# Late weight fetches, traced product order, single PSUM banks and early projection rows in a two-layer encoder trunk

## The chip, the cores and the metric

The kernel runs on one core of a Trainium2 chip. The metric is the device time of one execution in microseconds. A core has five engines with instruction queues of their own: TensorE (PE) does matmuls into PSUM, eight banks of 128 partitions x 512 fp32; VectorE (DVE), ScalarE (ACT) and GpSimd (POOL) work elementwise; SyncE (SP) issues the DMAs. Each engine works through its queue in the order in which it was written, and waits on semaphores for the others.

## The reference

The input is 1024 tokens of width 1024 in fp32. Two layers, each a mixer and an MLP with residuals, and a final RMSNorm:

```
for layer in range(2):
    mixer = even_mixer if layer == 0 else odd_mixer
    x = x + mixer(rmsnorm(x, g), ...)
    x = x + sq_relu_mlp(rmsnorm(x, g), w1, w2)     # u = relu(h @ w1); (u * u) @ w2, 4096 wide
return rmsnorm(x, g)
```

The even mixer is windowed attention beside a pooling mixer. The odd mixer is dense latent attention with 8 heads (`yc`, the first 512 channels) beside a gated recurrence (`yd`, the other 512), both concatenated and multiplied by `o_w_out` (1024 x 1024).

## The kernel before

Activations lie transposed, channels on the partitions, as tiles of 128 x 1024 (`G` tiles, 41 buffers); a half of one is `H2` or `U`. To keep fp32 accuracy each operand is split into a rounded part h and a rest l (`split`: a cast on ScalarE or POOL, a subtraction on VectorE or POOL), and each product runs three matmuls: h·h, h·l, l·h.

**Weights of the projections and of the MLP's last two pairs** go through one list, `wreq`, built by `requests` for all phases in order (L137), and two functions:

```
def weight(self, ahead=2):
    self.fetch(ahead + 1)
    return self.wout.pop(0)
```

`fetch` (L168) takes the next request, issues its DMA into one of two `raw` buffers, and splits it into two tiles of the tag `w`, of which there are eight. So when a phase takes its last weight, the first two of the next phase are already asked for. The tag `w` also holds the weight blocks of the MLP (`block("wb", ...)`, L272) and, in the odd attention, the transposed probabilities `cpT` (L1352) and the value tiles `VS` (L1317).

**The MLP** (`mlp`, L363) treats the 32 chunks of the hidden width in 16 pairs. 14 pairs use a seven-product scheme of 2 x 2 blocks (Strassen's kind), the last two (`TAIL`, pairs 14 and 15) do so only in the first products; their second products are plain and use four weights from `wreq` (L551). The first products of a pair go into four banks a, b, c, d: `head` writes a (B11), `rest` writes b (t2), c (t3), d (T1), then `second()` = `turn` calls `head2`, a second product into a (B21), then a second product into c (t4) and into d (B22). A product is 12 matmuls of 128 x 512. Between them VectorE and ScalarE read the banks: L396 copies a, L407 reads b, L410 and L419 read c, L412 and L424 read d, L401 reads a after `head2`. A second product into a bank must wait until the first result has been read. For the first six pairs (`NS`), `head` and `head2` run earlier, in a start stage, interleaved with the making of the operand blocks (`SNorm.late`, L1530), and `rest` follows for these six without `turn`. Pairs take two sets of banks in turn (`banks`, L284): four single-bank tiles of the pools `pb` and `pa`, or two double tiles `PS2` of the pool `p2`, cut into halves. `second` (L491) then runs the second products in three groups of pairs, seven steps per group, with `stream2` (weight blocks) and `tin` (hidden blocks read back from DRAM) prepared three ahead.

**The odd attention** (`odd`, L917) makes 128 steps u = 0 to 127, four for each of 32 (head, query pair): parts P (preparing a later head), S (scores of two query pairs ahead, in `PS2`), T (four transposes of probabilities to `cpT`) and V (`av`, the products with the values, `ODD_LAG` = 4 steps behind). After the loop the recurrence's output `yd` is split (L1164), the residual is loaded (`load_x`), the last four `av` run, `yc` is split, and then come the output rows: for each half n of the tokens and each of eight row blocks m, 24 matmuls over k = 4 to 7 (`yd`) and then k = 0 to 3 (`yc`).

**Order.** The source gives instructions in a traced order, but a planner with a cost model and the number of buffers of each tag reorders the instructions of every engine: an instruction that it thinks ready may pass earlier ones. `pin` (L111) ties an instruction behind the one traced before it on its engine. The numbers of buffers are kept as written; a tile waits until its buffer is free. `PS` (L92) hands out banks in rotation: two of `pb`, two of `pa`, and four halves of two `PS2` tiles; in `wide` mode the first four only.

Of the kernel before, what the change touches and what calls it, by code (L numbers as in the profile page):

```python
# [15 lines left out]
P = 128  # L16
S = 1024
# [29 lines left out]
class Trunk:  # L47
    def __init__(self, tc, a, pools, phases):
        self.tc, self.nc, self.a = tc, tc.nc, a
        self.cst, self.gp, self.wp, self.tp, self.sm, self.pb, self.pa, self.p2, self.dr = pools  # L50
# [10 lines left out]
        self.half = None  # L61
        self.halves = {}
        self.wreq = []
        self.wout = []
        for ph in phases:
            self.wreq += self.requests(ph)
# [21 lines left out]

    def PS2(self, name):
        return self.p2.tile([P, S], F32, tag="bb", name=self.nm(name))  # L90

    def PS(self, name):  # L92

        k = self.pk
        self.pk = (k + 1) % (4 if self.wide else 8)
        return self.PB(name) if k < 2 else self.PA(name) if k < 4 else self.PS2H(name)

    def PS2H(self, name):

        if self.half is None:  # L100
            self.half = self.PS2(name)
            return self.half[:, :N2]
        h, self.half = self.half, None
        return h[:, N2:]

    def set_wide(self, w):
        self.wide = w
        self.pk = 0
        self.half = None
# [27 lines left out]
    def requests(self, ph):  # L137
        a = self.a
        if ph == "even":
            r = [(a["e_w_in"][i], S) for i in (4, 5, 0, 1, 2, 3)] + [(a["e_w_pool"], N2)]  # L140
            r += [(a["e_w_in"][i], S) for i in (9, 8, 7, 6)]
            r += [(a["e_w_out"][1][m], S, "act", "pool") for m in range(4)]
            return r + [(a["e_w_out"][0][m], S) for m in range(4)]
        if ph == "odd":
            idx = {"xr3": 6, "ckv": 2, "cq0": 0, "cq1": 1, "xg0": 7, "xg1": 8, "xg2": 9, "xg3": 10}
            late = {"kn": (a["w_uk"], N2), "qr": (a["w_uq_r"], N2), "qn": (a["w_uq_n"], S), "vn": (a["w_uv"], N2)}
            r = [(a["o_w_in"][i], S, "act" if i != 5 else "pool") for i in (3, 4, 5)]
            seen = set()
            for op in ODD_START:
                k = op[:-1]  # L150
                if k in seen:
                    continue
                seen.add(k)
                if k in idx:
                    r.append((a["o_w_in"][idx[k]], S, "pool"))
                elif k in late:
                    r.append(late[k])
            return r + [(a["o_w_out"][m], S, "act", "pool") for m in range(NC)] * 2
        if ph == "final":
            return []  # L160
        l = int(ph[-1])
        return [(a["w2"][l, f], S) for p in TAIL for f in pair(p)]
# [5 lines left out]
    def fetch(self, ahead):  # L168

        while self.wreq and len(self.wout) < ahead:  # L170
            src, n, *eng = self.wreq.pop(0)
            raw = self.wp.tile([P, S], F32, tag="raw", name=self.nm("raw"), bufs=RAW_BUFS)
            self.nc.sync.dma_start(raw[:, :n], src)
            h = self.wp.tile([P, S], F32R, tag="w", name=self.nm("wh"))
            l = self.wp.tile([P, S], F32R, tag="w", name=self.nm("wl"))
            self.split(h[:, :n], l[:, :n], raw[:, :n], *eng)
            self.wout.append((h, l))

# [105 lines left out]
    def banks(self, which):  # L284
        if which:
            two = [self.PS2("q"), self.PS2("q")]
            return [x[:, s] for x in two for s in (slice(0, N2), slice(N2, S))]
        return [self.PB("q"), self.PB("q"), self.PA("q"), self.PA("q")]
# [74 lines left out]
    def mlp(self, l, nb, nxt, dram):  # L363
# [7 lines left out]
        def product(ps, blocks, first, last):  # L371
            w = stream.take()
            for c in range(4):
                x = blocks[c]
                cs = slice(c * P, (c + 1) * P)
                lo = slice(N2 + c * P, N2 + (c + 1) * P)
                for i, (a, b) in enumerate(((w[:, cs], x[:, :N2]), (w[:, cs], x[:, N2:]), (w[:, lo], x[:, :N2]))):
                    nc.tensor.matmul(ps, a, b, start=(first and c == 0 and i == 0), stop=(c == 3 and i == 2),  # L378
                                     skip_group_check=True)
# [12 lines left out]
        def head(p, ps):  # L392

            t1, u11 = self.U("t1"), self.U("u11")
            product(ps, nb.T["B11"], True, False)
            nc.scalar.copy(t1, ps)  # L396
            return t1, u11

        def head2(p, ps, u11):
            product(ps, nb.T["B21"], False, True)  # L400
            nc.scalar.activation(u11, ps, AF.Relu)  # L401
            nc.scalar.activation(u11, u11, AF.Square)
            put(p, "B11", u11)

        def rest(p, b, c, d, t1, u11, second=None):
            product(b, nb.T["t2"], True, False)
            V.tensor_tensor(t1, b, t1, op=ALU.add)  # L407
            product(c, nb.T["t3"], True, False)
            u22 = self.U("u22")
            V.tensor_tensor(u22, c, t1, op=ALU.subtract)  # L410
            product(d, nb.T["T1"], True, False)
# [5 lines left out]
            product(c, nb.T["t4"], False, True)  # L417
# [4 lines left out]
            product(d, nb.T["B22"], False, True)  # L422
# [30 lines left out]
        def turn(p, a, u11):  # L453
            head2(p, a, u11)
# [24 lines left out]
        for p in range(NS, NP):  # L479
            a, b, c, d = self.banks(k)  # L480
            k = 1 - k
            t1, u11 = head(p, a)
# [22 lines left out]
        for g, pairs in enumerate(GROUPS):  # L505
# [21 lines left out]
            A = self.banks(k)  # L527
            second(A, pairs, True, False)
# [388 lines left out]
    def odd(self, nb, xs, nxt):  # L917
# [217 lines left out]

        prep = iter(())
        for u in range(4 * NS):
            i, kk = divmod(u, 4)
            h, p = steps[i]
            for op in ODD_STEP:  # L1140
# [13 lines left out]
                elif op == "P":  # L1154
                    if p == 0 and kk == 0 and 1 <= h < 7:
                        prep = prep_qk(h + 1)
                    next(prep, None)
            if p == 1 and kk == 3 and h < 7:
                VS[h + 1] = self.head_values(h + 1, Vn)
        Yh, Yl = [None] * 8, [None] * 8  # L1160
        for c in range(4):
            Yh[4 + c], Yl[4 + c] = self.G("yh", F32R), self.G("yl", F32R)
            for s in H2:
                self.split(Yh[4 + c][:, s], Yl[4 + c][:, s], yd[c][:, s], "act", "pool")  # L1164
# [522 lines left out]
def trunk(tc, a, phases=("even", "mlp0", "odd", "mlp1", "final")):  # L1687
    PSUM = bass.MemoryType.PSUM
    with tc.tile_pool(name="cst", bufs=1) as cst, tc.tile_pool(name="sm", bufs=4) as sm, \
            tc.tile_pool(name="tp", bufs=4) as tp, tc.tile_pool(name="wp", bufs=W_BUFS) as wp, \  # L1690
            tc.tile_pool(name="gp", bufs=G_BUFS) as gp, tc.tile_pool(name="pb", bufs=2, space=PSUM) as pb, \
            tc.tile_pool(name="pa", bufs=2, space=PSUM) as pa, \
            tc.tile_pool(name="p2", bufs=2, space=PSUM) as p2, \
            tc.tile_pool(name="dr", bufs=1, space=bass.MemoryType.DRAM) as dr:
        t = Trunk(tc, a, (cst, gp, wp, tp, sm, pb, pa, p2, dr), phases)
# [116 lines left out]
```

## Time and profile before

| what | us |
|---|---|
| median of 3 runs (lowest to highest) | 2161.3 (2158.78 to 2161.65) |
| the profiled execution | 2161.66 |
| its span, first to last instruction | 2159.5 |
| TensorE busy with matmuls | 2051.3 (95%) |
| VectorE, ScalarE, POOL busy | 1542.9, 1065.0, 823.2 |
| mean granted TensorE clock | 0.987 of full speed |

In the profile, L498 is a line of the kernel; `q<-hb,wb` says that a tile named q was written from tiles hb and wb. "Idle before <-" names what ended the wait. The first MLP lies from about 310 to 950 us, its second products from about 650; the odd attention's steps from about 1180 to 1400, the odd output rows to 1490, the second MLP to about 2150.

### The profile page before, as it was taken

How to read it: one execution, taken by the hardware profiler on the slowest of the kernel's cores; microseconds unless marked ns; L12 is line 12 of the kernel's file. 1: busy time of each engine (PE TensorE's matmuls, PEld its weight loads, DVE VectorE, ACT ScalarE, POOL GpSimd, SP SyncE). 2: the span in 40 equal slices, each digit the busy share in tenths (PEclk: the TensorE clock that was granted, in tenths of full speed). 3: DMA queues.
4: the chain of work that ended last, by engine and by line, in shares of the span. 5: the costliest groups of instructions: out<-in, count | busy, mean ns of one | idle time of the engine just before them, and what ended most of it. 6: DMA issues, size and time to landing. Idle time of an engine off the chain costs nothing.

```text
span 2159.5 us, 27248 instructions
## 1 busy us (share of the span) xinstructions
PE 2051.3 (95%) x9600; PEld 1688.1 (78%) x9600; DVE 1542.9 (71%) x2365; ACT 1065.0 (49%) x1853; POOL 823.2 (38%) x635
## 2 busy tenths in 40 slices
PE   6989998999999999999997999999899999999997
PEld 5867776787777888888785898888678777788887
DVE  7688868765656877775898888717875655877964
ACT  5236645444544534340565777734645545544423
POOL 4133332332315142242557776463242321522414
PEclk9999999999999999999999999999999999999999
DMA  5630052543448535132102000245443445654302
GB/s 176 144 136 24 11 185 78 176 166 127 151 152 310 176 107 180 55 101 76 35 25 68 11 11 10 79 130 188 135 172 127 152 155 179 236 204 157 127 29 79
DMA packets 115544, 261.32 MB, mean 121 GB/s; under 512 B 19664, under 2 KB 21840, under 8 KB 115408
## 3 DMA queue, kind: packets, MB, share of 16 engines
q1 hardware_dynamic: 115408, 259.59, 35.7%
q8 instruction: 75, 1.23, 0.2%
q14 instruction: 61, 0.50, 0.1%
HBM read 178.28 MB, written 72.35 MB: 116 GB/s over the span
## 4 chain that ended last, share of the span: by engine, by line
PE 72%; DVE 12%; issue 5%; ACT 5%; DMA 3%; POOL 3%; SPq 0%; POOLq 0%; DVEq 0%; ACTq 0%
PE q L498 22%; PE q L378 22%; PE op L185 7%; PE z L185 6%; PE ms L1334 4%; PE o L185 3%; PE cav L1124 2%; PE ctp L1350 2%; DVE th L1443 1%; POOL acc L245 1%; DVE wb L130 1%; DMA X<-xm 1%; DMA raw<-in_e_w_in_dram 1%; PE tp L870 1%; DVE w L1433 0%
## 5 line engine op out<-in xcount | busy, mean ns | idle before, releaser
L378 PE MATMUL q<-hb,wb 128*128 128x512 f32 x2688 | 629.7, 394 | 34.6 <-DVE wb L130 9.8
L378 PEld LDWEIGHTS q<-hb,wb 128*128 128x128 f32 x2688 | 504.1, 189 | 158.2 <-DVE wb L130 12.8
L498 PE MATMUL q<-ub,wb 128*128 128x512 f32 x2352 | 539.3, 391 | 8.8 <-ACT wb L122 7.0
L498 PEld LDWEIGHTS q<-ub,wb 128*128 128x128 f32 x2352 | 443.2, 189 | 104.3 <-ACT wb L122 8.8
L130 DVE TENSOR_TENSOR wb<-raw,wb 128x512 fp32r<-128x512 f32 x268 | 226.6, 851 | 112.6 <-ACT wb L122 112.2
L122 ACT CAST wb<-raw 128x512 fp32r<-128x512 f32 x268 | 164.3, 619 | 183.0 <-PE q L378 112.7
L122 ACT CAST wb<-sum 128x512 fp32r<-128x512 f32 x152 | 93.8, 620 | 183.3 <-PE q L378 100.7
L130 DVE TENSOR_TENSOR ub<-ut,ub 128x512 fp32r<-128x512 f32 x168 | 136.3, 824 | 66.2 <-ACT ub L122 65.8
L122 ACT CAST ub<-ut 128x512 fp32r<-128x512 f32 x168 | 101.4, 618 | 147.2 <-DVE wb L130 18.8
L130 DVE TENSOR_TENSOR wb<-sum,wb 128x512 fp32r<-128x512 f32 x152 | 126.3, 833 | 22.5 <-ACT wb L122 21.5
L185 PE MATMUL z<-Hh,wh 128*128 128x512 f32 x328 | 129.8, 400 | 10.6 <-ACT wh L122 9.6
L245 POOL TENSOR_TENSOR acc<-acc,sq 128x512 f32<-128x512 f32 (+1 forms) x62 | 88.3, 1427 | 123.3 <-ACT sq L244 121.4
L185 PE MATMUL z<-Hl,wh 128*128 128x512 f32 x328 | 130.2, 397 | 4.1 <-DVE Hl L1471 4.0
L185 PE MATMUL z<-Hh,wl 128*128 128x512 f32 x328 | 129.1, 394 | 0.8 <-DVE wl L130 0.8
L323 POOL TENSOR_TENSOR sum<-raw,raw 128x512 f32<-128x512 f32 x28 | 40.3, 1448 | 215.6 <-DMA raw<-in_w_dram 184.4
L332 POOL TENSOR_TENSOR raw<-raw,raw 128x512 f32<-128x512 f32 x32 | 43.5, 1360 | 203.2 <-DVE wb L130 175.6
L1124 PE MATMUL cav<-cpT,VS 128*128 128x256 f32 x512 | 102.7, 305 | 3.6 <-ACT cpT L1353 2.3
L122 ACT CAST wh<-raw 128x1024 fp32r<-128x1024 f32 (+1 forms) x49 | 49.8, 1015 | 111.9 <-PE z L185 39.4
L1334 PE MATMUL ms<-Kt,Qt 128*128 128x512 f32 (+1 forms) x384 | 99.8, 396 | 2.2 <-ACT e L1341 1.4
L185 PE MATMUL op<-yh,wh 128*128 128x512 f32 x252 | 100.0, 398 | 1.4 <-DVE ya L887 0.9
L185 PE MATMUL op<-yl,wh 128*128 128x512 f32 x252 | 98.9, 393 | 0.0
L185 PE MATMUL op<-yh,wl 128*128 128x512 f32 x252 | 98.0, 393 | 0.0
(343 smaller groups left out, 3815.0 us busy)
## 6 DMA issues: line engine op xcount, KB each, us to landing
raw<-in_w_dram SPq DMA_DIRECT2D x140, 512.0 KB, 4.5
xm<-X SPq DMA_DIRECT2D x32, 256.0 KB, 2.0
X<-xm SPq DMA_DIRECT2D x16, 512.0 KB, 6.6
raw<-in_o_w_out_dram SPq DMA_DIRECT2D x16, 512.0 KB, 3.5
raw<-in_o_w_in_dram SPq DMA_DIRECT2D x11, 512.0 KB, 3.5
raw<-in_e_w_in_dram SPq DMA_DIRECT2D x10, 512.0 KB, 5.1
X<-in_x_dram SPq DMA_DIRECT2D x16, 256.0 KB, 5.6
raw<-in_e_w_out_dram SPq DMA_DIRECT2D x8, 512.0 KB, 3.6
```

The lines of the kernel that those rows point to most:

```text
L122: self.nc.scalar.copy(out, x)
L130: e.tensor_tensor(out, x, y, op=ALU.subtract)
L185: self.nc.tensor.matmul(ps, l, r, start=(first and i == 0), stop=(last and i == n - 1))
L245: (eng or nc.gpsimd).tensor_tensor(acc, acc, sq, op=ALU.add)
L323: add(x, blk(p, 1, 0), blk(p, 1, 1), op=ALU.add)
L332: add(x, x, blk(p, 1, 0), op=ALU.add)
L378: nc.tensor.matmul(ps, a, b, start=(first and c == 0 and i == 0), stop=(c == 3 and i == 2), skip_group_check=True)
L498: nc.tensor.matmul(ps[m], a, b, start=(first and j == 0 and i == 0), stop=(j == len(pairs) - 1 and i == 2), skip_group_check=True)
L870: nc.tensor.transpose(tp[:, h * P:(h + 1) * P], pt[h // 2][:, o:o + P], self.ident)
L1124: nc.tensor.matmul(ACC[0][:, (p % 2) * 256:(p % 2 + 1) * 256], VS[h][:, kb * P:(kb + 1) * P], pp[:, t * N2 + ii * 256:t * N2 + (ii + 1) * ...
L1334: nc.tensor.matmul(ps[:, s], l[rows, qs], r[rows, s], start=(i == 0), stop=(i == 2))
L1350: nc.tensor.transpose(tp[:, (2 * i + j) * P:(2 * i + j + 1) * P], pr[j][:, kb * P:(kb + 1) * P], self.ident)
```

## The change

1. The lists of requests get a mark `None` ahead of the MLP's last-pair weights and ahead of the odd output weights. `fetch` stops there; `release(n, late)` takes the mark away, fetches n weights and pins the first `late` DMAs. It is called in the MLP's last group before its fifth step, and in the odd attention after step u = 112.
2. The first products of `rest`, of `turn` and of the later `head`s are pinned: each product's first matmul stays behind the one traced before it.
3. A pool `pc` of four single banks takes the place of the `PS2` halves in `banks` and in `PS`. `PS2` stays for scores, gates and the new early rows.
4. In the odd attention the splits of `yd` move into steps 96 to 111 (one half tile every two steps), the weights of row blocks 0 to 3 for k = 4 to 7 are loaded and split by themselves in steps 105 to 117, and the 48 matmuls of these rows for the first half of the tokens are traced from step 120 on, into two `PS2` tiles. The later fetch of these four weights takes only the other half, and the row loop skips the first part for them.

```
+    def PC(self, name):
+        return self.pc.tile([P, N2], F32, tag="c", name=self.nm(name))
...
-        return self.PB(name) if k < 2 else self.PA(name) if k < 4 else self.PS2H(name)
+        return self.PB(name) if k < 2 else self.PA(name) if k < 4 else self.PC(name)
...
-            return r + [(a["o_w_out"][m], S, "act", "pool") for m in range(NC)] * 2
+            return r + [None] + [(a["o_w_out"][m][:, :N2], N2, "act", "pool") for m in range(4)] + \
+                [(a["o_w_out"][m], S, "act", "pool") for m in [*range(4, NC), *range(NC)]]
...
-        return [(a["w2"][l, f], S) for p in TAIL for f in pair(p)]
+        return [None] + [(a["w2"][l, f], S) for p in TAIL for f in pair(p)]
...
         while self.wreq and len(self.wout) < ahead:
+            if self.wreq[0] is None:
+                break
...
-            self.nc.sync.dma_start(raw[:, :n], src)
+            d = self.nc.sync.dma_start(raw[:, :n], src)
+            if self.late > 0:
+                self.late -= 1
+                self.pin(d)
...
+    def release(self, n, late=0):
+
+        assert self.wreq.pop(0) is None
+        self.late = late
+        self.fetch(n)
...
-            two = [self.PS2("q"), self.PS2("q")]
-            return [x[:, s] for x in two for s in (slice(0, N2), slice(N2, S))]
+            return [self.PC("q") for _ in range(4)]
...
-                    nc.tensor.matmul(ps, a, b, start=(first and c == 0 and i == 0), stop=(c == 3 and i == 2),
-                                     skip_group_check=True)
+                    m = nc.tensor.matmul(ps, a, b, start=(first and c == 0 and i == 0), stop=(c == 3 and i == 2),
+                                         skip_group_check=True)
+                    if pin and c == 0 and i == 0:
+                        self.pin(m)
...
-            product(b, nb.T["t2"], True, False)
+            product(b, nb.T["t2"], True, False, True)
...
-            head2(p, a, u11)
+            head2(p, a, u11, True)
...
-            t1, u11 = head(p, a)
+            t1, u11 = head(p, a, True)
...
+            if g == len(GROUPS) - 1:
+                self.release(2, 2)
             second(A, pairs, True, False)
...
+        def y_split(c, s):
+            if s.start == 0:
+                Yh[4 + c], Yl[4 + c] = self.G("yh", F32R), self.G("yl", F32R)
+            self.split(Yh[4 + c][:, s], Yl[4 + c][:, s], yd[c][:, s], "act", "pool")
+
+        def out_weights(m):
+            raw = self.H2("owr", "owr")
+            dma(raw, a["o_w_out"][m][:, N2:])
+            w = self.G("ow", F32R)
+            self.split(w[:, :N2], w[:, N2:], raw, "act", "pool")
+            early[m] = [w]
+
+        def out_early():
+            two = [self.PS2("op"), self.PS2("op")]
+            for m in range(4):
+                w = early[m][0]
+                ps = two[m % 2][:, (m // 2) * N2:(m // 2 + 1) * N2]
+                early[m].append(ps)
+                for k in range(4):
+                    cs, lo = slice(k * P, (k + 1) * P), slice(N2 + k * P, N2 + (k + 1) * P)
+                    self.mm3(ps, [(w[:, cs], w[:, lo], Yh[4 + k][:, H2[0]], Yl[4 + k][:, H2[0]])], k == 0, False)
+                    if k % 2:
+                        yield
...
+                    if 96 <= u < 112 and u % 2 == 0:
+                        y_split((u - 96) // 4, H2[u // 2 % 2])
+                    if 104 <= u < 120 and u % 4 == 1:
+                        out_weights((u - 104) // 4)
+                    if u >= 120:
+                        next(fill, None)
...
+            if u == 112:
+                self.release(2, 2)
...
+        for _ in fill:
+            pass
...
-                grp = [(m0 + j, self.PS("op")) for j in range(2)]
-                for part in range(2):
+                ready = n == 0 and m0 < 4
+                grp = [(m0 + j, early[m0 + j][1] if ready else self.PS("op")) for j in range(2)]
+                for part in range(1 if ready else 0, 2):
...
+            tc.tile_pool(name="pc", bufs=4, space=PSUM) as pc, \
```

The other products of `rest` get the same fifth argument.

More of the change, by code (lines that the diff above doesn't have):

```diff
@@ L49, in __init__ @@
         self.tc, self.nc, self.a = tc, tc.nc, a
-        self.cst, self.gp, self.wp, self.tp, self.sm, self.pb, self.pa, self.p2, self.dr = pools
+        self.cst, self.gp, self.wp, self.tp, self.sm, self.pb, self.pa, self.pc, self.p2, self.dr = pools
         nc = self.nc
@@ L60, in __init__ @@
         self.pk = 0
-        self.half = None
         self.halves = {}
@@ L64, in __init__ @@
         self.wout = []
+        self.late = 0
         for ph in phases:
@@ L95, in PS @@
         self.pk = (k + 1) % (4 if self.wide else 8)
-        return self.PB(name) if k < 2 else self.PA(name) if k < 4 else self.PS2H(name)
[L98 to L104, printed above, removed]
+        return self.PB(name) if k < 2 else self.PA(name) if k < 4 else self.PC(name)
     def set_wide(self, w):
@@ L108, in set_wide @@
         self.pk = 0
-        self.half = None
     def pin(self, ins):
@@ L369, in mlp, with product @@
         stream = nb.stream
-        def product(ps, blocks, first, last):
+        def product(ps, blocks, first, last, pin=False):
             w = stream.take()
@@ L390, in put, with head, head2 @@
             spill[p, k] = d
-        def head(p, ps):
+        def head(p, ps, pin=False):
             t1, u11 = self.U("t1"), self.U("u11")
-            product(ps, nb.T["B11"], True, False)
+            product(ps, nb.T["B11"], True, False, pin)
             nc.scalar.copy(t1, ps)
             return t1, u11
-        def head2(p, ps, u11):
-            product(ps, nb.T["B21"], False, True)
+        def head2(p, ps, u11, pin=False):
+            product(ps, nb.T["B21"], False, True, pin)
             nc.scalar.activation(u11, ps, AF.Relu)
@@ L405, in rest @@
         def rest(p, b, c, d, t1, u11, second=None):
-            product(b, nb.T["t2"], True, False)
+            product(b, nb.T["t2"], True, False, True)
             V.tensor_tensor(t1, b, t1, op=ALU.add)
-            product(c, nb.T["t3"], True, False)
+            product(c, nb.T["t3"], True, False, True)
             u22 = self.U("u22")
             V.tensor_tensor(u22, c, t1, op=ALU.subtract)
-            product(d, nb.T["T1"], True, False)
+            product(d, nb.T["T1"], True, False, True)
             V.tensor_tensor(u22, d, u22, op=ALU.add)
@@ L416, in rest @@
                 second()
-            product(c, nb.T["t4"], False, True)
+            product(c, nb.T["t4"], False, True, True)
             u21 = self.U("u21")
@@ L421, in rest @@
             put(p, "B21", u21)
-            product(d, nb.T["B22"], False, True)
+            product(d, nb.T["B22"], False, True, True)
             u12 = t1
@@ L1134, in av @@
                                         tmp[0:64], op=ALU.add)
+        Yh, Yl = [None] * 8, [None] * 8
+        early = {}
+        def y_split(c, s):
[19 more added lines that the diff above has]
+                        yield
+        fill = out_early()
         prep = iter(())
@@ L1157, in odd @@
                     next(prep, None)
+            if u == 112:
+                self.release(2, 2)
             if p == 1 and kk == 3 and h < 7:
                 VS[h + 1] = self.head_values(h + 1, Vn)
[L1160 to L1164, printed above, removed]
         X = self.load_x(xs)
@@ L1692, in trunk @@
             tc.tile_pool(name="pa", bufs=2, space=PSUM) as pa, \
+            tc.tile_pool(name="pc", bufs=4, space=PSUM) as pc, \
             tc.tile_pool(name="p2", bufs=2, space=PSUM) as p2, \
             tc.tile_pool(name="dr", bufs=1, space=bass.MemoryType.DRAM) as dr:
-        t = Trunk(tc, a, (cst, gp, wp, tp, sm, pb, pa, p2, dr), phases)
+        t = Trunk(tc, a, (cst, gp, wp, tp, sm, pb, pa, pc, p2, dr), phases)
         gains = {"even": "e_norm", "odd": "o_norm", "mlp0": "mlp0", "mlp1": "mlp1"}
```

## Prediction

> **What bounds the kernel now.** I read the page first, then a table by stage, then the waits of TensorE inside the stages, then single instants. On the page, PE is TensorE's matmuls and PEld its weight loads:
>
> ```profile
> span 2159.5 us, 27248 instructions
> PE 2051.3 (95%) x9600; PEld 1688.1 (78%) x9600; DVE 1542.9 (71%) x2365; ACT 1065.0 (49%) x1853; POOL 823.2 (38%) x635
> ```
>
> TensorE carries the kernel. Its 9600 matmuls stay 9600, so the change can only remove time in which TensorE waits or runs slowly. The table by stage gives window, length, then busy time and count of instructions for PE, PEld, DVE, ACT and POOL, and last the granted clock, the DMA share and GB/s:
>
> ```profile
> 331.00:334.00 3.00, 3.00 (x9) 2.30 (x8) 1.25 (x5) 0.00 (x0) 0.77 (x1) 0.51 0.00 0
> 311.00:374.00 63.00, 53.18 (x210) 41.27 (x211) 53.22 (x86) 34.44 (x66) 16.07 (x8) 0.92 0.33 122
> 374.00:420.00 46.00, 43.09 (x188) 34.76 (x187) 35.66 (x45) 21.25 (x36) 19.06 (x14) 1.00 0.49 164
> 420.00:640.00 220.00, 215.50 (x938) 174.68 (x937) 131.04 (x182) 107.96 (x178) 61.55 (x45) 1.00 0.42 146
> 640.00:700.00 60.00, 54.88 (x229) 43.39 (x228) 38.05 (x44) 28.44 (x51) 29.55 (x20) 0.97 0.84 306
> 700.00:960.00 260.00, 260.00 (x1149) 215.33 (x1148) 199.90 (x273) 109.27 (x187) 76.57 (x50) 1.00 0.36 119
> 890.00:920.00 30.00, 30.00 (x134) 24.82 (x134) 20.91 (x29) 8.17 (x13) 6.50 (x4) 1.00 0.00 1
> 1340.00:1380.00 40.00, 39.05 (x264) 35.14 (x263) 33.59 (x63) 29.56 (x56) 16.11 (x20) 1.00 0.04 14
> 1381.00:1402.50 21.50, 17.87 (x117) 15.04 (x117) 16.03 (x25) 17.93 (x35) 11.87 (x10) 0.92 0.45 172
> 1490.00:1544.00 54.00, 48.26 (x207) 37.99 (x205) 45.72 (x71) 30.69 (x57) 12.18 (x6) 0.97 0.30 104
> 1600.00:1820.00 220.00, 213.05 (x922) 171.71 (x922) 129.49 (x179) 107.01 (x177) 57.16 (x42) 1.00 0.42 148
> 1820.00:1870.00 50.00, 45.49 (x191) 36.50 (x191) 35.09 (x36) 23.50 (x42) 31.30 (x20) 0.97 0.92 329
> ```
>
> From 700 to 960 us (the second products of the first MLP and what follows) nothing waits: 1149 matmuls in 260 us, one each 226 ns. That is my measure for the other MLP windows. In the first products' even run, 220 us would hold 972 matmuls; 420 to 640 holds 938 and 1600 to 1820 holds 922. So 34 and 50 matmuls are missing, 7.7 and 11.3 us, together 19.0 us. Only 4.5 and 6.95 us of that is PE standing idle; the rest is the slow refill behind each stall.
>
> **The change, part by part.** The sum starts from the profiled execution's own time, 2161.66 us (span 2159.5); the median of the runs, 2161.3, is 0.4 us under it.
>
> *A. First products in traced order, on single banks.* The waits of PE in the two even runs (total us, times, longest), and a row from the list over the whole kernel:
>
> ```profile
> PE q L378 <- DVE t L407: 3.1, 4, 0.8
> PE q L378 <- DVE wb L130: 1.0, 1, 1.0
> ```
> ```profile
> PE q L378 <- DVE t L407: 3.9, 5, 0.8
> PE q L378 <- DVE wb L130: 1.9, 2, 1.0
> PE q L378 <- DVE u L412: 0.9, 1, 0.9
> ```
> ```profile
> PE q L378 <- DVE u L410: 6.8, 8, 1.4
> ```
>
> L407 reads bank b. No later product of the pair writes b, so why does PE wait for it? The timeline of one stall tells (start, length, then what):
>
> ```profile
> 479.09 39.00 PE L378 MATMUL q<-hb,wb 128*128 128x512 f32 x168 [0.79 <-DVE t L407]
> ```
> ```profile
> 482.71 0.59 ACT L401 ACTIVATE t<-q 128x512 f32<-128x512 f32 x1
> ```
>
> The product that starts at 479.09 ends one product (12 x 226 ns = 2.7 us) later, and what reads it, held up by one cast, is L401: it is `head2`, the second product into bank a. The planner put it straight behind b's product, though the source has it after c and d. Where the banks come as two halves of a `PS2` tile, a and b share a tile; the waits come in one pair of two, the ones on `PS2`. I read this as a wait for the tile, not for the bank. The change removes both causes: order is pinned, and each bank is its own tile. Late next would be the second products into c and d, which need L410 and L412; in traced order two products (5.4 us) lie between, against a 0.7 us subtraction on a VectorE busy 131 of 220 us. I let the L407 and L412 waits go, 7.9 us, and the 2.9 us on `wb` stay: 7.9 / 10.8 of 19.0 us is 14 us. Bounds: 19 us, and a loss if L410 comes late everywhere (below). The six start pairs already run five products between waits on L410; I leave them at nothing.
>
> *B. Four more weight slots in the MLP's start.* `weight()` looks two ahead, so the MLP's last-pair weights are cast before the MLP begins:
>
> ```profile
> 300.03 1.05 ACT L122 CAST wh<-raw 128x1024 fp32r<-128x1024 f32 x1 [3.34 <-PE op L185]
> ```
>
> Two weights with halves h and l hold four of the eight `w` slots until the MLP's end, which leaves four to the `wb` blocks. In 420 to 640 ScalarE's casts of `wb` wait for PE to give a slot back:
>
> ```profile
> ACT wb L122 <- PE q L378: 80.9, 53, 3.2
> ```
>
> PE doesn't feel it there, but in the start it does. PE's waits in 311 to 374, then in 1490 to 1544, and the stretch after one of them:
>
> ```profile
> PE q L378 <- DVE wb L130: 4.3, 2, 3.4
> PE q L378 <- ACT t L396: 2.4, 2, 2.0
> PE q L378 <- ACT wb L122: 1.6, 2, 0.9
> ```
> ```profile
> PE q L378 <- DVE wb L130: 2.6, 1, 2.6
> PE q L378 <- ACT t L396: 1.8, 2, 1.4
> PE q L378 <- ACT wb L122: 1.1, 2, 0.7
> ```
> ```profile
> 330.69 4.14 PE L378 MATMUL q<-hb,wb 128*128 128x512 f32 x10 [0.98 <-DVE wb L130]
> ```
>
> Waits on `wb` are 5.9 us in the first MLP and 3.7 in the second. After the stall at 330.69 the granted clock is 0.51 (first window row) and ten matmuls take 4.14 us, not 2.4: 1.7 us more. Two such spells in the first MLP's start (3.4 us) and 0.03 x 54 = 1.6 us in the second follow these waits. With eight slots the blocks are ready before the VectorE rush, so up to 5.9 + 3.4 + 3.7 + 1.6 = 14.6 us could go. But VectorE is busy 53.2 of 63 and 45.7 of 54 us, and the first pair can't finish before VectorE has made the operand blocks: earlier `wb` splits must fit its idle 9.8 and 8.3 us. The low end is nothing; I take the middle, 7.3 us.
>
> The Trainium skill (TensorE: Matmul & The Clock Gate, section "HAM oscillation — how this bites in real kernels") has the rule that idle gaps of TensorE up to about 3.4 us don't cost clock. By that rule the slow spells aren't tied to these waits, B would be half of 9.6 us, 4.8, and the sum 2136. The trace differs: the clock halved right behind a gap of 0.98 us, so I keep the spells.
>
> The two fetches (two DMAs, two casts, two subtractions per MLP) move from the crowded start to the last group's fifth step, 12 products or 32 us before the second products end. There (890 to 920) VectorE is busy 20.9 of 30 us, ScalarE 8.2, and DMA near nothing; PE doesn't wait. Pinned on SP, each DMA goes behind the operand reads already queued; it waits for a `raw` buffer that is long free, so nothing queues up behind it. Without this cover two casts and subtractions would cost some 4 us. The third and fourth weights get their slots from the last `wb` blocks, as before.
>
> *C. Early rows in the attention's drain.* Two output-projection weights are cast here and hold four slots through the attention:
>
> ```profile
> 1157.57 1.07 ACT L122 CAST wh<-raw 128x1024 fp32r<-128x1024 f32 x1
> ```
>
> Once the scores are done, TensorE has only transposes and value products left. Groups of PE from 1381 to 1402.5, then one step inside the attention:
>
> ```profile
> L1124 PE MATMUL cav<-cpT,VS 128*128 128x256 f32 x61 | 13.4, 329 | 3.6 <-ACT cpT L1353 2.3 <-DVE cpT L1354 1.2
> L1350 PE MATMUL ctp<-ident,e 128*128 128x128 f32 x56 | 9.2, 291 | 0.0
> ```
> ```profile
> 1230.76 0.60 PE L1350 MATMUL ctp<-ident,e 128*128 128x128 f32 x4
> 1231.12 0.72 PE L1124 MATMUL cav<-cpT,VS 128*128 128x256 f32 x4
> 1231.68 0.60 PE L1350 MATMUL ctp<-ident,e 128*128 128x128 f32 x4
> ```
>
> A step of four and four takes 0.92 us when it runs free. The drain's 14 steps and five more value products should take 13.5 us and take 21.5: 8.0 us lost, with ScalarE busy 17.9 of 21.5. The change puts 4 x 4 x 3 = 48 projection matmuls, 10.9 us, into that hole instead of behind it, and moves eight casts out of it:
>
> ```profile
> L122 ACT CAST yh<-th 128x512 fp32r<-128x512 f32 x8 | 4.6, 628 | 0.0
> ```
>
> PE then has 13.5 + 10.9 = 24.4 us of work where hole and rows took 32.4. I take 7 of the 8 us. The casts go to steps 96 to 111, with four more of the same size for the early weights: 12 x 0.63 = 7.5 us on ScalarE, which from 1340 to 1380 is busy 29.6 of 40. It fits, barely; POOL, busy 16.1, takes the subtractions. Wider slots for `cpT` help the same stretch, whose PE idle is 0.95 us. Bounds for both together: 1 us gained, up to 7.5 lost; I take nothing. Four DMAs become eight of half size on a queue 4% busy; the last rows' weights reuse slots as they did. What is late next is the residual, whose loads SP issues from 1388.4 on:
>
> ```profile
> X<-xs SPq DMA_DIRECT2D x7, 512.0 KB, 7.5
> ```
>
> Seven land by 1401; with the drain 7 us shorter the first is wanted near 1398 and then one each 2.7 us, so they still come in time, unless the four tiles of early weights hold back their buffers (1 or 2 us, taken as nothing).
>
> *Elsewhere.* The rotating banks of the other projections (`z`, `op`, `o`) become four single tiles in place of two double ones. The pools now name twelve banks where they named eight, so where single and double tiles meet (around the even attention, the gates, the drain) one kind waits for the other, as the halves of a double tile do now. Without a row that parts the two I bound it by a stall of the present kind, 0.8 us either way at each of some five places, and take nothing.
>
> Sum: 14 + 7.3 + 7 = 28.3 us; 2161.7 - 28.3 = 2133 us.
>
> **The rivals.**
> *Only A works.* VectorE keeps the start (53.2 of 63 us busy speaks for it) and ScalarE, now nearly full before the drain, gives half of C back: 14 + 3.5, 2144 us.
> *Every stall goes.* A 19, B 14.6, C 8, and the switch to second products, where 229 and 191 matmuls stand for 265 and 221 (15 us short), gives half of it: 49 us, 2113 us. Against it: DMA runs there at 0.84 and 0.92, and nothing of the change feeds it faster.
> *The pins cost time (slower).* PE can no longer step past a late L410 or L412. Each of 32 pairs has two such places, 64. The eight waits on L410 now average 0.85 us; at all 64 that is 54 us, 48 more than the 6.8 now, against 28 gained: 2181 us. It decides from 0.55 us per place. For it: VectorE runs 35.7 of 46 us in the start pairs. Against it: 5.4 us of slack in the even run.
> *No change.* The bank waits turn into equal `wb` waits and B into waits for operand blocks: 2161 us.
>
> **How the numbers follow.** Forecast (2124 to 2140 us) 0.51; only A 0.22; every stall 0.12; no change 0.06; slower 0.09. The range 2112 to 2150 holds the first three and leaves out 0.15 and some tails. About 0.2% (4.3 us) is what a measurement can tell: faster 0.85, same 0.06, slower 0.09.
>
> **What would show it.** A: no PE wait on L407, and some 965 matmuls in each 220 us of the even run. B: no cast `wh<-raw` at the MLP's start, waits on `wb` there under 2 us, fewer half-clock spells. C: `op` matmuls between `ctp` and `cav`, and the projection ending some 7 us earlier relative to the last scores. Wrong would be: L410 or L412 at the head of PE's waits, ScalarE full and PE waiting on `cpT` or `e` in the last heads, or a later start of the second products that eats the gain.

## The result

| | us, median (lowest to highest) | ratio to before, 95% interval |
|---|---|---|
| before | 2161.3 (2158.8 to 2161.7) | |
| after | 2120.7 (2117.3 to 2122.9) | 0.9818 [0.9806, 0.9830] |
| predicted | 2133 (2112 to 2150) | 0.987 |

The change takes 40 us off, 12 more than forecast. The profiled execution of the changed kernel took 2122.9 us, its span is 2120.8. Its page:

```profile
span 2120.8 us, 27226 instructions
PE 2033.4 (96%) x9600; PEld 1691.6 (80%) x9600; DVE 1569.7 (74%) x2365; ACT 1051.5 (50%) x1857; POOL 831.3 (39%) x639
```

As many matmuls as before, in 39 us less. Where, says this table: each stage ends at a matmul that can be found in both traces (first or last of a group; of an MLP the 144th matmul of its first products, which is the last of the six pairs' `head` and `head2`, and the 240th matmul of its second products), in us of the profiled executions.

| stage | term | before | after | difference |
|---|---|---|---|---|
| start to the first product of MLP 0 | elsewhere | 311.2 | 304.4 | -6.8 |
| to the 144th matmul of its first products | B | 53.6 | 48.5 | -5.1 |
| to the 240th matmul of its second products | A | 347.3 | 342.3 | -5.0 |
| to the first `z` of the odd mixer | | 255.7 | 255.7 | 0.0 |
| to the last score `ms` | elsewhere | 411.4 | 409.6 | -1.8 |
| to the last `op` | C | 113.5 | 104.9 | -8.6 |
| to the 144th matmul of MLP 1's first products | B | 42.8 | 41.5 | -1.3 |
| to the 240th matmul of its second products | A | 349.2 | 340.3 | -8.9 |
| to the end | elsewhere | 274.9 | 273.7 | -1.2 |

By the forecast's terms that is A 13.9 (14 forecast), B 6.4 (7.3), C 8.6 (7), elsewhere 9.8 (0). It looks as if three terms were right and one overlooked. The experiments say otherwise for two of the three.

The windows of the changed kernel that answer to those of before (columns as there): start and even run of MLP 0, the switch to its second products, the drain, start, even run and switch of MLP 1.

```profile
304.40:367.40 63.00, 52.08 (x208) 41.05 (x207) 56.76 (x86) 35.23 (x67) 18.38 (x9) 0.89 0.30 110
400.00:620.00 220.00, 220.00 (x972) 182.19 (x972) 156.99 (x190) 103.22 (x182) 66.34 (x45) 1.00 0.45 156
629.20:689.20 60.00, 52.52 (x215) 41.92 (x214) 43.59 (x53) 28.21 (x51) 29.77 (x20) 0.94 0.73 272
1360.50:1391.20 30.70, 30.57 (x187) 26.59 (x187) 17.15 (x28) 15.60 (x30) 5.60 (x5) 1.00 0.45 170
1465.00:1519.00 54.00, 46.94 (x204) 37.46 (x203) 42.84 (x68) 29.14 (x55) 13.17 (x8) 0.96 0.23 81
1560.00:1780.00 220.00, 220.00 (x972) 182.26 (x971) 153.96 (x187) 104.86 (x185) 65.13 (x45) 1.00 0.44 154
1783.00:1833.00 50.00, 44.16 (x179) 35.18 (x178) 35.57 (x39) 23.45 (x42) 30.70 (x20) 0.93 0.87 309
```

The even runs are full: 972 matmuls in 220 us, where before had 938 and 922. The drain is dense, 30.57 of 30.70 us. The switches are worse than before: 215 matmuls in the 60 us from the first second product, where 265 would fit and the kernel before had 234. PE's waits at the switch of MLP 0:

```profile
PE q L505 <- ACT wb L116: 3.9, 3, 2.7
PE q L505 <- DVE ub L124: 3.6, 1, 3.6
```

### The profile page after: what moved, and what is told of

Same layout as the page of the kernel before. It is cut to its first block, busy times and chain, and to the rows that moved or that the text cites. A ratio compares the mean times of both kernels' runs of the same rounds, so it can differ in the third digit from the quotient of the medians.

```text
span 2120.8 us, 27226 instructions
## 1 busy us (share of the span) xinstructions
PE 2033.4 (96%) x9600; PEld 1691.6 (80%) x9600; DVE 1569.7 (74%) x2365; ACT 1051.5 (50%) x1857; POOL 831.3 (39%) x639
## 4 chain that ended last, share of the span: by engine, by line
PE 76%; DVE 9%; issue 6%; ACT 3%; DMA 3%; POOL 3%; SPq 0%; POOLq 0%; ACTq 0%; DVEq 0%
PE q L383 25%; PE q L505 23%; PE z L191 7%; PE op L191 6%; PE ms L1378 4%; PE cav L1133 3%; PE o L191 3%; PE ctp L1394 3%; DMA raw<-in_w_dram 1%; DVE th L1487 1%; PE av L887 1%; PE tp L879 1%; DVE wb L124 1%; POOL acc L251 1%; DVE wl L124 0%
## 5 line engine op out<-in xcount | busy, mean ns | idle before, releaser
L383 PE MATMUL q<-hb,wb 128*128 128x512 f32 x2688 | 622.0, 394 | 16.8 <-ACT t L403 10.2
L383 PEld LDWEIGHTS q<-hb,wb 128*128 128x128 f32 x2688 | 509.4, 190 | 127.7 <-ACT t L403 12.6
L124 DVE TENSOR_TENSOR wb<-raw,wb 128x512 fp32r<-128x512 f32 x268 | 248.9, 942 | 51.1 <-ACT wb L116 51.1
L124 DVE TENSOR_TENSOR ub<-ut,ub 128x512 fp32r<-128x512 f32 x168 | 130.1, 788 | 57.1 <-ACT ub L116 56.3
L124 DVE TENSOR_TENSOR wb<-sum,wb 128x512 fp32r<-128x512 f32 x152 | 145.7, 960 | 30.0 <-ACT wb L116 29.8
L347 POOL TENSOR_TENSOR sum<-sum,raw 128x512 f32<-128x512 f32 x32 | 50.0, 1564 | 257.1 <-DVE wb L124 257.1
L389 ACT ACTIVATE u<-u 128x512 f32<-128x512 f32 x64 | 40.5, 633 | 197.6 <-DVE u L419 151.1
L1398 DVE TENSOR_TENSOR cpT<-ctp,cpT 128x512 fp32r<-128x512 f32 x128 | 87.0, 687 | 18.1 <-ACT cpT L1397 16.3
L191 PE MATMUL op<-yh,wh 128*128 128x512 f32 x240 | 95.2, 399 | 2.9 <-ACT wh L116 1.5
L1382 DVE TENSOR_REDUCE cmx<-ms 128x1 f32<-128x1024 f32 x64 | 78.2, 1223 | 21.3 <-PE ms L1378 20.8
```

The source lines that it names most:

```text
L124: e.tensor_tensor(out, x, y, op=ALU.subtract)
L191: self.nc.tensor.matmul(ps, l, r, start=(first and i == 0), stop=(last and i == n - 1))
L347: add(x, x, blk(p, 0, 1), op=ALU.add)
L383: m = nc.tensor.matmul(ps, a, b, start=(first and c == 0 and i == 0), stop=(c == 3 and i == 2), skip_group_check=True)
L1382: nc.vector.reduce_max(mx, ps, axis=AX.X)
L1398: nc.vector.tensor_tensor(pp[:, N2:], tp, pp[:, :N2], op=ALU.subtract)
```

## The experiments

All ratios are to the kernel before, run on the same chip beside it, in five rounds.

| kernel | us | ratio, 95% interval |
|---|---|---|
| before + banks of the rotation | 2153.0 | 0.9970 [0.9959, 0.9980] |
| before + order | 2185.1 | 1.0116 [1.0100, 1.0131] |
| before + late MLP weights | 2203.9 | 1.0203 [1.0189, 1.0217] |
| before + early rows, late odd weights | 2162.5 | 1.0010 [1.0001, 1.0019] |
| before + all single banks | 2136.5 | 0.9885 [0.9871, 0.9898] |
| before + all single banks + order | 2125.4 | 0.9842 [0.9828, 0.9855] |
| after without late MLP weights | 2119.3 | 0.9812 [0.9798, 0.9825] |
| after without order | 2121.5 | 0.9824 [0.9810, 0.9837] |
| after without the MLP's single banks | 2175.3 | 1.0071 [1.0058, 1.0084] |
| after, residual loads (X) later | 2117.5 | 0.9805 [0.9792, 0.9819] |
| after, X later, without late MLP weights | 2117.4 | 0.9806 [0.9793, 0.9820] |
| after, X later, four blocks ahead | 2113.7 | 0.9783 [0.9770, 0.9797] |

**One part alone, on the kernel before.** First the rotation's banks:

```
-        return self.PB(name) if k < 2 else self.PA(name) if k < 4 else self.PS2H(name)
+        return self.PB(name) if k < 2 else self.PA(name) if k < 4 else self.PC(name)
```

> The kernel before, with four single PSUM banks in place of the two double tiles in the rotation of the projections (z, op, o) alone; the banks of the MLP's products, their order, the weights and the early rows are as before. Theory: the 11 us that the changed kernel gains outside the MLP and the drain (7 us before the first MLP, 4 us between its end and the odd scores) are this part's: about 2150 us, the even scores first at 133 us (140 before), and odd z to odd scores 4 us shorter. Rival 1: the start alone is this part's and the stretch ahead of the odd scores belongs to another part: 2154 us. Rival 2: the start is early but a later wait takes it back: within 2 us of 2161.

0.9970, 6.5 us. That is nearer to rival 1; its profile gains 3.4 us before MLP 0 and 1.3 between `z` and the last score. It also gains 4.2 and 2.3 us in the start stages of the two MLPs, where no expectation looked: their `head`s take their banks from the rotation. The waits of PE from 30 to 60 us, in this kernel and then in the changed one:

```profile
PE z L190 <- DVE vt L604: 3.8, 1, 3.8
PE rb L236 <- DVE rr L216: 1.6, 1, 1.6
```
```profile
PE rb L237 <- DVE rr L217: 1.7, 1, 1.7
PE ss L226 <- POOL acc L251: 0.5, 1, 0.5
```

PE's instructions stand in the same order in both down to the first products of MLP 0. What differs is what a `z` tile waits for: in the one kernel a result that VectorE reads late (L604), in the other none. In the kernel with all single banks and the order (below) every engine runs the same instructions in the same order as here up to the end of MLP 0's start stage, VectorE reads that result at 42.90 us against 42.88 here, and PE doesn't wait for it; MLP 0 begins at 303.0 us there and at 307.8 here. So the rest of the gain before MLP 0 doesn't come from another order of instructions. That the `z` tile lies in another bank is my reading; the traces don't name banks.

Then the order, the pins of `product` alone:

> The kernel before, with the MLP's first products pinned in traced order and nothing else; two banks still share a double tile. Theory (the order is what removes the wait: head2 no longer stands behind b's product, so a shared tile costs nothing): the waits on L407 are gone, the two even runs lose 12 us together, and the whole comes to about 2149 us, less what the switch to second products gives back. Rival (the shared tile is what costs, the order alone moves the wait to c and d, which share a tile as well): waits on L410 or L412 take the place, a gain under 4 us, 2157 to 2163 us.

1.0116, 25 us slower: neither figure; the mechanism is the rival's, a wait that moves to other readers, only larger. PE's waits from 440 to 660 us (where L413 copies a, L424 reads b, L427 and L436 read c, as L403, L414, L417 and L426 in the changed kernel), one stall, and VectorE at that place:

```profile
PE q L393 <- ACT t L413: 6.0, 5, 1.2
PE q L393 <- DVE u L427: 4.0, 5, 0.8
PE q L393 <- DVE u L436: 3.5, 4, 0.9
PE q L393 <- DVE t L424: 1.4, 1, 1.4
```
```profile
523.53 8.50 PE L393 MATMUL q<-hb,wb 128*128 128x512 f32 x36 [0.78 <-DVE u L427]
```
```profile
522.79 0.69 DVE L427 TENSOR_TENSOR u<-q,t 128x512 f32<-128x512 f32 x1 [1.10 <-PE q L393]
```

In traced order b comes right behind a and d right behind c, and each of these twos is one tile of before: d's product waits until c has been read, b's until a has been copied. The waits come in fours and fives, one per pair on double tiles.

Late MLP weights alone (the `None` ahead of the MLP's requests and its `release`):

> The kernel before, with the last-pair weights of the MLPs fetched in the last group's fifth step and nothing else. Theory (the slots alone feed the start): first product to 144th 5 us shorter in the first MLP, 3 us in the second, 2153 us. Rival (VectorE's operand blocks set the start, and the slots help only with products in the new order): starts within 1 us of before, 2160 us. A second rival: the casts that move to the end of the MLP stall PE there, 2163 us.

1.0203, 43 us slower, which neither theory foresaw. The second rival's place is not it: 255.7 us from the 240th second product to `z`, as in every kernel here. The loss is in the first products:

```profile
PE q L393 <- ACT t L413: 9.4, 4, 2.4
PE q L393 <- DVE wb L134: 4.7, 3, 2.2
PE q L393 <- DVE t L424: 3.4, 4, 0.9
```

With other buffers the planner laid out another order, and it waits on the readers of a and b (L413, L424), as the pinned one does, and longer on each copy of a. Why the planner chose this order is not shown.

Early rows with the late odd weights:

> The kernel before, with the early rows and the late weights of the odd output projection and nothing else. Theory: last score to the end of the odd projection 6 us shorter, the rest unmoved, 2155 us. Rival (the gain needs the single banks of the rotation, because early rows sit in the double tiles that the rotation uses too): waits at the first rows behind the drain, a gain under 2 us, 2160 us.

1.0010, no gain: the rival's size, by another mechanism. The drain is as dense as forecast, 33.07 of 33.20 us, but MLP 1 gives it back in one wait (windows, then PE's timeline, then ScalarE's):

```profile
1376.80:1410.00 33.20, 33.07 (x198) 28.32 (x197) 18.03 (x30) 17.27 (x32) 7.86 (x7) 1.00 0.44 164
```
```profile
1517.35 4.51 PE L394 MATMUL q<-hb,wb 128*128 128x512 f32 x12 [14.43 <-ACT t L414]
```
```profile
1515.04 0.62 ACT L126 CAST hb<-t 128x512 fp32r<-128x512 f32 x1 [10.86 <-DVE t L1596]
1516.19 0.62 ACT L126 CAST hb<-t 128x512 fp32r<-128x512 f32 x1 [0.53 <-DVE t L1596]
1516.71 0.58 ACT L414 COPY t<-q 128x512 f32<-128x512 f32 x1
```

PE waits for a copy of 0.58 us that stands in ScalarE's queue behind casts which wait 10.9 us for VectorE's operand blocks.

**Parts together.** Single banks with the order, without late weights and early rows:

> The changed kernel without the late weights and without the early rows: traced order and single banks only (part A, with the rotation). Since the order alone cost 23 us in its profile, with waits on L413, L427 and L436, each behind the bank that shares a tile with the one wanted: Theory (single banks and order work only together): those waits are gone, the even runs lose 0.1 us in 20, the whole is 12 us for A and 7 for the rotation under before, 2141 us. Rival (the even run needs the slots as well, since four slots hold back wb): waits on wb in the even runs, 2150 us or more.

0.9842, 34 us; much more than the theory's 19. The order, which cost 25 us on double tiles, gains on single banks (0.9842 against 0.9885 for the next kernel, 9 us). Then single banks alone:

```
-            two = [self.PS2("q"), self.PS2("q")]
-            return [x[:, s] for x in two for s in (slice(0, N2), slice(N2, S))]
+            return [self.PC("q") for _ in range(4)]
```

> The kernel before, with single PSUM banks alone (the MLP's products and the rotation); order, weights and early rows as before. The changed kernel without its pins took 2121.5 us, without its late MLP weights 2119.3, without late weights and early rows 2125.4. Theory (the single banks carry the even run and the starts by themselves): 2124 to 2128 us, no wait on L407's successor in the even runs, second products from 629 us on. Rival (with neither pins nor late weights the planner orders the run as badly as with the late weights alone): 2150 us or more, waits on t in the even runs.

0.9885, 25 us, between the two expectations. Its even runs:

```profile
400.00:620.00 220.00, 220.00 (x971) 181.88 (x971) 141.97 (x192) 113.17 (x186) 68.58 (x48) 1.00 0.43 153
1570.00:1790.00 220.00, 220.00 (x973) 182.15 (x972) 141.44 (x193) 111.75 (x184) 63.67 (x45) 1.00 0.43 154
```

They are as full as the changed kernel's, with no pin: with single banks the planner itself issues the products as a, b, c, d, a, c, d, the traced order. So `head2` behind b's product came with the shared tile. Against the rotation's banks alone (0.9970) the MLP's single banks are worth 18 us here. What the order adds on top lies outside the even runs: 3.9 and 1.5 us in the six start pairs of the two MLPs, where PE waits here on L416, the reader of c, 8.9 us in six waits. Another 2.5 us before MLP 0 and 3.4 us between `z` and the last score lie where no pin stands; I put them down to the placement above, and no run shows it.

The changed kernel with the MLP's products back on double tiles:

> The changed kernel with the MLP's products back on halves of double tiles; the rotation stays single, and order, late weights and early rows stay. Theory (the order and the late weights each pay only for the coupling of two banks in a tile that they make worse, 25 and 44 us when alone): 2185 us or more, with waits on L403, L417 and L426, each a reader of the neighbouring half. Rival 1 (they don't add up): 2165 to 2180 us. Rival 2 (the gain of the changed kernel comes from the rotation's banks, by what they free): 2130 us or less.

1.0071: rival 1 in size, the theory's mechanism (L403, L417 and L426 are L404, L418 and L427 in this kernel). Against 0.9818 the MLP's single banks are worth 2.5%, 55 us, inside the change, more than the whole change. PE's waits over the whole kernel, then its even runs:

```profile
PE q L384 <- ACT t L404: 18.2, 14, 4.6
PE q L384 <- DVE u L418: 10.1, 11, 2.3
```
```profile
420.00:640.00 220.00, 208.39 (x894) 167.67 (x894) 136.50 (x174) 99.71 (x171) 56.78 (x41) 0.99 0.38 137
1600.00:1820.00 220.00, 208.39 (x895) 167.65 (x894) 135.68 (x174) 97.33 (x167) 56.74 (x41) 0.99 0.38 138
```

The changed kernel without the pins, and without the late MLP weights:

> The changed kernel without the pins; single banks, late weights and early rows stay. Theory (once each bank is a tile of its own, a head2 behind b's product waits for nothing, so the order adds little): within 4 us of the changed kernel, 2117 to 2125 us. Rival (the order is needed, as the late weights alone re-plan the run for the worse, by 43 us): waits on L403 and L414 in the even runs, 2135 to 2160 us.

> The changed kernel, with the MLP's last-pair weights fetched ahead of the MLP again. Theory (the slots are worth what part B was forecast at): each MLP start 3 to 5 us longer and nothing else, 2128 us. Rival 1 (the start is set by VectorE's operand blocks, and ScalarE's copies queue behind their casts): 2121 us. Rival 2 (in the new order the four slots also hold up the even runs): wb waits there, 2140 us.

0.9824 and 0.9812 against 0.9818: neither part moves the time beyond what these intervals tell, with the other and the early rows in place. The first is as its theory said; the 9 us that the order gained without late weights and early rows are not seen beside them, and no run tells which of the two makes that so. The second is at the figure of its rival 1, but by another way: without late weights MLP 1's start is 3.4 us longer (44.9 against 41.5) and MLP 0's 1.0 (49.5 against 48.5; one profile says no more than about 2.6 there, as the kernel before and the one with the order alone, which run the same instructions in the same order up to there, took 53.6 and 51.0), but the stretches from there to the 240th matmul of the second products are 4.6 and 3.2 us shorter (337.7 and 337.1 against 342.3 and 340.3). What four more slots give in the start, they take at the switch. VectorE there, with late weights and then without:

```profile
660.70 7.45 DVE L124 TENSOR_TENSOR wb<-raw,wb 128x512 fp32r<-128x512 f32 x5
668.08 3.44 DVE L124 TENSOR_TENSOR ub<-ut,ub 128x512 fp32r<-128x512 f32 x2
```
```profile
661.87 2.39 DVE L124 TENSOR_TENSOR wb<-raw,wb 128x512 fp32r<-128x512 f32 x2
664.18 1.77 DVE L124 TENSOR_TENSOR ub<-ut,ub 128x512 fp32r<-128x512 f32 x1
665.88 1.78 DVE L124 TENSOR_TENSOR wb<-raw,wb 128x512 fp32r<-128x512 f32 x1
667.59 3.48 DVE L124 TENSOR_TENSOR ub<-ut,ub 128x512 fp32r<-128x512 f32 x2
```

With free slots five weight subtractions stand ahead of the `ub` block that PE wants next; with four slots, two. Early rows are the step from single banks with the order (0.9842) to this kernel (0.9812): 6.5 us, give or take about 4.

**Further on the switch.** The residual loads, eight of 512 KB per MLP, stand ahead of operand loads on SP. They are traced one step later and pinned:

```
-            if g == 0:
-                load(range(4, 8))
             second(B, pairs, True, False)
+            if g == 0:
+                load(range(4, 8))
...
-            if g == 0:
-                load(range(4))
             second(A, pairs, False, True)
+            if g == 0:
+                load(range(4))
```

> The changed kernel, with the eight 512 KB residual loads of each MLP issued one step of the second products later (behind the operand loads that they now stand ahead of). The changed kernel loses 11.6 us at the first switch to second products and 9.8 at the second, with DMA 0.78 to 0.89 busy. Theory (the loads of X hold up the weights wanted first): most of the loss goes, 2106 to 2112 us. Rival 1 (all the bytes are wanted in that stretch, the wait only moves): waits on X or raw some 20 us later, 2119 to 2123 us. Rival 2 (the stores of the last pair at the head of the queue hold up the loads): 2119 to 2121 us, with the same waits on wb.

0.9805 against 0.9818, intervals overlapping: not told apart from the changed kernel, and between its theory and its rivals. In the profile the stretches to the 240th matmul of the second products are 2.8 and 3.0 us shorter, but in MLP 1 only 0.9 of the 3.0 lies at the switch and the rest in the start pairs. The waits on `wb` are gone but for 0.4 us, and in each MLP one of 5.6 us on `ub` has come: now PE waits for VectorE. The same without late weights, and with late weights and `W_AHEAD` 4 in place of 3:

> The changed kernel with the residual loads one step later and the MLP's last-pair weights fetched early again, as these two gave 2117.5 and 2119.3 us each. Theory (both small gains are real and in different places: at the switch, and at the start of the MLP): 2114 to 2116 us. Rival (the difference of the run without late weights is chance): 2117 to 2118 us.

> The changed kernel with the residual loads one step later, and the second products' blocks prepared four ahead in place of three. With the loads later, PE still waits 5.6 us for a ub block at 659 us, where DVE is busy 10.0 of 10.0 us and its subtractions take 1.5 to 1.8 us beside POOL's sums against 0.68 without them. Theory (VectorE, slowed beside POOL, is what the switch waits for, and looking further ahead gives it no time): within 3 us of 2117. Rival (the operands are only asked for too late): both switches lose 4 us less, 2109 us.

The first came out as its rival said, 2117.4: the two small gains don't add up, though its waits on `ub` at the switch of MLP 0 fell from 5.6 to 2.4 us and it has the shortest switches of all. The second, 0.9783, is the fastest kernel of all, and its interval lies clear of the changed kernel's: 0.35%, 7.5 us. At 2113.7 us it just misses its theory's range and is far from its rival. What fed it is not settled: it still waits 5.0 and 4.8 us for `ub`, as the theory said, its switches are 2.0 and 1.5 us shorter than with the later loads alone, and its interval overlaps that of the later loads alone.

## Why the prediction was right or wrong

**A, 14 us forecast, 13.9 in its stage; the cause was half right, and the size is luck.** "I read this as a wait for the tile, not for the bank" held. "The change removes both causes" failed: there was one cause. The order was a consequence of the tile, and goes when the tile goes. It showed as forecast: 972 matmuls instead of "some 965", and no wait on the reader of b. But two misses cancel in the 13.9. To see them, the even run's end must be set rightly: in the kernel before, 16 matmuls of the second products run ahead of the last first product, 3.6 us per MLP.

```profile
647.70 3.79 PE L498 MATMUL q<-ub,wb 128*128 128x512 f32 x16
651.33 2.88 PE L378 MATMUL q<-hb,wb 128*128 128x512 f32 x12
```

From the 504th matmul to the last of the first products the changed kernel takes 190.6 us in each MLP; the kernel before takes 203.3 and 204.4, without these 16 matmuls 199.7 and 200.8. So the even runs gained 9.1 and 10.2 us, together 19.3: the forecast's upper bound, refill and `wb` waits included, where it had let the `wb` waits stay. The switches, from the last first product to the 240th second matmul and with the 16 counted in, went from 61.7 and 61.4 to 66.0 and 64.2 us, 4.3 and 2.8 longer, and the forecast's sum has no term for that. It is not A that costs this. With banks and order but without late weights the switches take 62.2 and 61.9 us, and with everything but the late MLP weights 61.8 and 60.9. So what A lost in its stage is B's price: in the kernel with banks and order alone A's stages gained 8.9 and 12.3 us, 21.2 in place of 14.

**The rival of the pins** ("PE can no longer step past a late L410 or L412") was real, under a condition that the forecast didn't name: with two banks in a tile the pins cost 25 us alone, at the reader of c that it names (L427 there) and more at that of a (L413), which it doesn't. With single banks its counter-argument holds ("5.4 us of slack in the even run"), and they cost nothing.

**B, 7.3 us forecast; its stages gained 6.4, but not from the slots.** The rotation's banks alone already gain 4.2 and 2.3 there, as do banks and order without any late weight (49.4 and 40.4 us); of the 4.2, up to 2.6 may be the spread of one profile. The step that failed is "with eight slots the blocks are ready before the VectorE rush": beside banks, order and early rows the slots gave 1.0 and 3.4 us, the 3.4 where the early rows had made MLP 1's start longer (40.4 to 44.9 us), and 7.8 were lost up to the 240th matmul of the second products, nearly all at the switch. The forecast looked only at the start for what the slots feed. In the whole, B is worth nothing (0.9818 with it, 0.9812 without). Nor did the forecast see that the low end was "nothing" only on single banks: on double tiles the slots cost 43 us. Waits on `wb` fell to 2.3 us in MLP 0, where the forecast said "under 2 us", and to none in MLP 1, and new waits took their place, with VectorE busy 56.8 of 63 us:

```profile
PE q L383 <- ACT t L403: 5.2, 2, 4.6
PE q L383 <- DVE u L417: 2.3, 1, 2.3
PE q L383 <- DVE wb L124: 2.3, 2, 1.8
PE rb L237 <- DVE rr L217: 1.2, 1, 1.2
```

The forecast of "fewer half-clock spells" failed too: the granted clock of the two start windows is 0.89 and 0.96, before it was 0.92 and 0.97. Two spells of the changed kernel, the second just behind the start stage, and the gaps of PE ahead of them:

```profile
326.60:330.00 3.40, 3.40 (x12) 2.73 (x11) 2.22 (x4) 0.59 (x1) 0.00 (x0) 0.51 0.00 0
364.20:367.60 3.40, 3.40 (x10) 2.61 (x9) 3.36 (x5) 2.95 (x6) 1.29 (x1) 0.50 0.38 153
```
```profile
325.79 1.33 PE L237 MATMUL rb<-ident,rr 128*128 128x128 f32 x8 [1.15 <-DVE rr L217]
363.51 11.85 PE L383 MATMUL q<-hb,wb 128*128 128x512 f32 x44 [2.30 <-DVE u L417]
```

A slow spell again came within 1 us behind a short gap, here of 1.15 us. The rule of the Trainium skill that was weighed in the prediction (TensorE: Matmul & The Clock Gate, section "HAM oscillation — how this bites in real kernels": gaps up to about 3.4 us cost no clock) doesn't agree with these rows either. Whether the gap alone sets off the spell is not shown: the small matmuls of the norm (`rb`, 128x128) stand beside the first, and the waits of 0.8 us in the even run before left the clock at 1.00.

**C, 7 us forecast, 8.6 in its stage, about 6.5 in the whole.** Right in size and mechanism: the hole is full, at 0.13 us idle. "ScalarE full" didn't come true (15.6 of 30.7 us). What the forecast left out is the condition: alone, the rows gain nothing, since the time they save is lost at MLP 1's start, behind ScalarE's queue. Even on single banks they make that start 4.5 us longer when the late MLP weights are not there.

**Elsewhere, 0 +- 4 us forecast, 9.8 came,** 6.8 of it before the first MLP. This is most of the 12 us miss. The term was mis-sized by treating the rotation as a few stalls of 0.8 us: the planner lays out anew every stage that uses the pool, and one wait of 3.8 us came or went with the order unchanged (by the bank that a tile landed in, as I read it). The bound also missed that the MLPs' start stages use the rotation, so that most of B's 6.4 us belongs here too. The ten kernels with all or part of the single banks reach MLP 0 after 303.0 to 307.8 us, the four with none after 308.6 to 311.5.

## What to carry to other kernels

Two accumulators that share a tile are one for whoever waits on the tile: look which readers' names stand behind PE's waits, and give each accumulator a tile of its own before touching the order, since an order pinned over shared tiles can cost more than it was to bring. Parts of a change to a planned kernel don't add up: here two parts that cost 25 and 43 us alone cost nothing once a third was in, and a stage that came out at its forecast held a larger gain and another part's loss, so measure each with the others in place. More buffers for one stream let it run ahead of another on the engine they share; look at the next stage's first operand before giving them.

## What the runs showed of the hardware

VectorE's subtraction of two 128x512 tiles takes 0.64 to 0.69 us by itself and 1.7 us beside POOL's sums. VectorE, then POOL, in the kernel with the later X loads:

```profile
663.27 5.12 DVE L124 TENSOR_TENSOR ub<-ut,ub 128x512 fp32r<-128x512 f32 x3
668.31 1.28 DVE L525 TENSOR_TENSOR X<-q,X 128x512 f32<-128x512 f32 x2
669.51 1.28 DVE L124 TENSOR_TENSOR wb<-raw,wb 128x512 fp32r<-128x512 f32 x2
```
```profile
664.42 5.10 POOL L344 TENSOR_TENSOR raw<-raw,sum 128x512 f32<-128x512 f32 x3
```

Three of each run in step, 1.71 and 1.70 us apiece, as if they took turns. `X<-q,X`, which takes one operand from PSUM, is not held up: it starts at 668.31, beside the last sum, and two take 1.28 us, as two subtractions do once POOL is done. The Trainium skill (SBUF — State Buffer, section "SBUF: two separate sides") has VectorE operations with two SBUF inputs and GpSimd operations exclude each other for a whole instruction, and these rows agree in the main: 1.71 us is less than 0.64 and the 1.29 that a sum takes beside an idle VectorE in the same trace, so some part of the two still overlaps. It matters here: at the switch VectorE is the engine PE waits for, and each sum on POOL holds up a VectorE that has no time to spare by about 1.71 - 0.64 = 1.07 us.
